# The gate's second product made of float32r parts in the large projections' banks

## The chip, the cores and the metric

The kernel runs on one core of a Trainium2 chip. The metric is the device time of one execution in microseconds (us). TensorE does matrix products, VectorE and ScalarE do elementwise work and read the products' banks (PSUM), GpSimd helps with elementwise work, and SyncE issues most of the loads. In the rows of the profile they are called PE, DVE, ACT, POOL and SP. PEld is TensorE's weight load.

## What is computed

Two layers of an encoder are applied to 768 rows (512 of one sequence, 256 of another) with a model width of 1024. Layer 0 runs differential attention and a bidirectional RWKV-7 mixer side by side, layer 1 runs dilated attention, and each layer ends with a SwiGLU network. The change touches one line of the RWKV mixer, the output gate g:

```python
GATE_LORA = 160
RWKV_WIDTH = RWKV_HEADS * HEAD_DIM          # 512

def rwkv_mixer(xn, r_p, k_p, v_p):
    ...
    xg = xn + xx * mu_g
    ...
    g = (jax.nn.sigmoid(xg @ g1) @ g2).astype(f32)
    ...
    return ((y + bonus.reshape(B, S, H * N)) * g).astype(xn.dtype)
```

The gate's hidden row has 160 columns. The kernel keeps them in two tiles, 128 of them in `hg` and 32 in `hh`, each with all 768 rows of the input along its free dimension.

## The kernel before

Large products are made of float32r parts. `split` makes two float32r tiles of a float32 tile: the high part is a cast on ScalarE (line 139), the low part is the remainder, a subtraction on VectorE (line 140). A product is then three float32r products, high by high, high by low and low by high. Small products are done in float32 directly (line 84).

A scheduler sets the order of each engine's instructions when the program is built. Line 83 gives every float32r product the lowest rank there is, so that it is put where nothing else is ready: it is filler. Each engine then works off its own list in order, and waits on semaphores for what it needs.

The work around the change is the method `rkv`, at about 20 to 365 us. For each of four blocks of 128 columns (j) it projects k, v and r, makes the operands of the RWKV recurrence in both directions (`operands`: tiles `AL`, `KB` and others, on VectorE, GpSimd and ScalarE), multiplies `AL` with `KB` in groups of 64x64 products (bank `pr`), and ScalarE copies the results to the tiles `G`. Each full `G` is inverted by `invert`: VectorE transposes it and solves 31 rows one after another (lines 752 and 754, here called the row chain), and TensorE makes 32x32 products in the bank `iv`, with ScalarE copies `Hs` and `Tif`/`Tib` between them. There are three such inversions. The last one needs the last `pr` products and is still running while the differential attention has begun.

`stage` makes the decays and rates of a block from their hidden tiles (bank `st`, one bank). `bonus` makes small products with `rk` (bank `pr`), which VectorE copies to `bon` (line 693). At the end of `rkv` come the gates' first projections (`gates`, names g and h), then `gate_out`, which makes g, and then `values`, which projects the values of the attention: six tiles of 24 float32r products in the banks `gm`, of which there are four. Weights go through five pairs of tiles `wh`/`wl` (`slot`) and two load tiles `wraw`.

After `rkv` follow the projections and scores of the differential attention (`diff_qk`, `diff_attention`), whose first product is a `gm<-xh,wh` at 365.45 us.

Of the kernel before, what the change touches and what calls it, by code (L numbers as in the profile page):

```python
# [18 lines left out]
P = 128  # L19
D = 1024  # L20
T = 768
# [33 lines left out]
class Core:  # L55
# [461 lines left out]
    def gate_out(self, hp, park):  # L517

        nc = self.nc
        g2b = self.pads[self.npad % 2][0:32, 0:512]  # L520
        nc.sync.dma_start(g2b, self.A["g2b"])
        for t in range(NT):
            o = self.bank("st")
            self.mm(o, self.hid["g"][:, t * P:(t + 1) * P], self.g2[0], True, False)
            self.mm(o, self.hid["h"][:, t * P:(t + 1) * P], g2b, False, True)
            g = self.big(("vv", "s", "sq")[t % 3])[:, 0:512]
            nc.scalar.copy(out=g, in_=o)
            nc.scalar.dma_start(park["g"][t], g)
# [1133 lines left out]
```

## Time and profile before

| | us |
|---|---|
| median of 3 runs | 2114.9 (2113.24 to 2115.16) |
| the profiled execution, device time | 2114.44 |
| the profiled execution, span of its instructions | 2112.6 |
| mean granted clock of TensorE over the span | 0.975 |

The device time is 1.8 us longer than the span from the first to the last instruction. The granted clock is a share of the full rate: 1.00 is 2.4 GHz, 0.50 is 1.2 GHz, and a value between them is a mean over a stretch that had both.

### The profile page before, as it was taken

Reading aid. Unit: us, or ns where it says so; the run is one execution under the profiler, and the core shown is the slowest. Engines: PE = TensorE matmul, PEld = TensorE weight load, DVE = VectorE, ACT = ScalarE, POOL = GpSimd, SP = SyncE. Lnnn points to the kernel's source line nnn. Section 1 sums busy time; section 2 is a strip of 40 time slices with the busy share of each in tenths; the row PEclk is TensorE's granted clock in tenths of the full one; section 3 lists DMA queues with packets and bytes.
Section 4 is the critical chain, followed back from the end, with each engine's and each line's share of the span. In section 5 each row is a group of like instructions: output and inputs, shape, how many; then the busy total and the mean of one; then the engine's idle time right before and its main releaser. Section 6 shows DMA issues by size and latency. Waiting matters only on the chain. (4 is left out here: it accounts for less than half of the span.)

```text
span 2112.6 us, 33740 instructions
## 1 busy us (share of the span) xinstructions
PE 2043.2 (97%) x13282; PEld 1768.4 (84%) x13282; DVE 1383.5 (65%) x2161; ACT 901.6 (43%) x1699; POOL 866.7 (41%) x819
## 2 busy tenths in 40 slices
PE   7999999999999999999999999999998999999998
PEld 7767676777887778999999998888687999999997
DVE  5456996846579577566666658544569566666665
ACT  5466565446655254433333335222445433333332
POOL 3344341543113137543443545553227434543442
PEclk9989997989999999999999999999899999999999
DMA  4334434214356212211122145320121222211124
GB/s 156 83 73 91 94 74 126 79 26 124 98 160 190 111 69 81 80 60 60 60 80 80 61 139 178 90 82 29 61 110 61 80 73 67 79 61 60 60 80 150
DMA packets 150227, 189.01 MB, mean 89 GB/s; under 512 B 95926, under 2 KB 107784, under 8 KB 150068
## 3 DMA queue, kind: packets, MB, share of 16 engines
q1 hardware_dynamic: 126880, 168.00, 25.6%
q10 hardware_dynamic: 20372, 12.03, 2.0%
q0 software_dynamic: 2816, 6.83, 1.1%
q8 instruction: 104, 1.70, 0.3%
q14 instruction: 55, 0.45, 0.1%
HBM read 150.20 MB, written 36.23 MB: 88 GB/s over the span
## 5 line engine op out<-in xcount | busy, mean ns | idle before, releaser
L83 PE MATMUL gm<-xh,w 128*128 128x384 f32 x864 | 236.1, 337 | 3.7 <-DVE sil L340 3.7
L140 DVE TENSOR_TENSOR wl<-wraw,wh 128x1024 fp32r<-128x1024 f32 (+1 forms) x96 | 125.5, 1308 | 156.3 <-ACT wh L139 153.2
L83 PE MATMUL gm<-T,w 128*128 128x384 f32 x1080 | 212.0, 339 | 6.1 <-DVE w L140 3.1
L83 PE MATMUL gm<-xh,wh 128*128 128x256 f32 (+3 forms) x640 | 207.9, 347 | 0.8 <-ACT pad L503 0.8
L83 PE MATMUL gm<-xl,wh 128*128 128x256 f32 (+3 forms) x640 | 206.7, 346 | 0.0
L83 PE MATMUL gm<-xh,wl 128*128 128x256 f32 (+3 forms) x640 | 205.3, 345 | 0.0
L83 PEld LDWEIGHTS gm<-T,w 128*128 128x128 f32 x1080 | 191.8, 188 | 11.9 <-DVE w L140 4.3
L140 DVE TENSOR_TENSOR w<-S,w 128x512 fp32r<-128x512 f32 x174 | 172.4, 991 | 40.9 <-ACT w L139 33.6
L139 ACT CAST wh<-wraw 128x1024 fp32r<-128x1024 f32 (+1 forms) x103 | 107.5, 1045 | 173.0 <-PE gm L83 103.1
L139 ACT CAST w<-S 128x512 fp32r<-128x512 f32 x174 | 107.8, 621 | 151.4 <-POOL S L299 56.7
L139 ACT CAST w<-wraw 128x512 fp32r<-128x512 f32 x126 | 76.0, 620 | 210.1 <-PE gm L83 141.3
L83 PEld LDWEIGHTS gm<-xh,w 128*128 128x128 f32 x864 | 158.1, 188 | 8.5 <-DVE sil L340 4.3
L83 PE MATMUL sc<-xh,w 128*128 128x384 f32 x544 | 150.5, 337 | 4.6 <-DVE xl L140 3.0
L140 DVE TENSOR_TENSOR w<-wraw,w 128x512 fp32r<-128x512 f32 x126 | 118.3, 955 | 41.3 <-ACT w L139 40.9
L303 POOL TENSOR_TENSOR S<-wraw,S 128x512 f32<-128x512 f32 x42 | 62.2, 1481 | 202.7 <-DVE w L140 202.7
L83 PE MATMUL gm<-xl,w 128*128 128x384 f32 x432 | 145.2, 336 | 0.0
L83 PEld LDWEIGHTS gm<-xh,wh 128*128 128x128 f32 (+1 forms) x640 | 119.7, 193 | 21.6 <-issue 5.8
L83 PEld LDWEIGHTS gm<-xh,wl 128*128 128x128 f32 (+1 forms) x640 | 118.9, 193 | 20.6 <-issue 7.4
L83 PEld LDWEIGHTS gm<-xl,wh 128*128 128x128 f32 (+1 forms) x640 | 119.0, 193 | 20.1 <-issue 7.7
L406 DVE TENSOR_TENSOR acc<-acc,ob 128x512 f32<-128x512 f32 x128 | 87.5, 684 | 63.4 <-PE ob L83 62.4
L358 POOL TENSOR_TENSOR sil<-sil,v 128x384 f32<-128x384 f32 x44 | 47.3, 1075 | 166.8 <-DVE v L340 166.4
L83 PE MATMUL ob<-wl,hh 128*128 128x512 f32 x288 | 113.5, 394 | 0.0
(511 smaller groups left out, 5279.6 us busy)
## 6 DMA issues: line engine op xcount, KB each, us to landing
wraw<-in_gate SPq DMA_DIRECT2D x44, 512.0 KB, 3.4
wraw<-in_down SPq DMA_DIRECT2D x44, 512.0 KB, 3.8
wraw<-in_up SPq DMA_DIRECT2D x40, 512.0 KB, 3.4
wraw<-in_wqk SPq DMA_DIRECT2D x20, 512.0 KB, 3.7
wraw<-in_wo SPq DMA_DIRECT2D x14, 512.0 KB, 4.1
wraw<-in_wrkv SPq DMA_DIRECT2D x12, 512.0 KB, 3.5
KB<-pkKB SPq DMA_DIRECT2D x24, 256.0 KB, 3.3
pkx<-x SPq DMA_DIRECT2D x12, 512.0 KB, 3.2
```

Source lines behind the costliest of these rows:

```text
L83: return self.nc.tensor.matmul(o, a, b, start=start, stop=stop)
L139: self.nc.scalar.copy(out=hi, in_=x)
L140: (eng or self.nc.vector).tensor_tensor(out=lo, in0=x, in1=hi.bitcast(F32), op=ALU.subtract)
L303: eng.tensor_tensor(out=s2, in0=a12, in1=s2, op=ALU.subtract)
L358: nc.gpsimd.tensor_tensor(out=o, in0=o, in1=a[0], op=ALU.mult)
L406: nc.vector.tensor_tensor(out=accs[t][:, fs], in0=accs[t][:, fs], in1=os[t, f], op=ALU.add)
```

## The change

`gate_out` splits the two hidden tiles and the two parts of the weight g2 into float32r parts, in three pairs of weight tiles, and makes each tile of g from six float32r products, in a bank `gm` and with the filler's rank, in place of two float32 products in the bank `st`. Copies and stores of g stay.

```diff
         g2b = self.pads[self.npad % 2][0:32, 0:512]
         nc.sync.dma_start(g2b, self.A["g2b"])
+        hg, hh, w = (self.slot() for _ in range(3))
+        self.split(*(x[:, :T] for x in hg), self.hid["g"])
+        self.split(*(x[:, 0:512] for x in w), self.g2[0])
+        self.split(*(x[0:32, :T] for x in hh), self.hid["h"])
+        self.split(*(x[0:32, 512:D] for x in w), g2b)
         for t in range(NT):
-            o = self.bank("st")
-            self.mm(o, self.hid["g"][:, t * P:(t + 1) * P], self.g2[0], True, False)
-            self.mm(o, self.hid["h"][:, t * P:(t + 1) * P], g2b, False, True)
+            o = self.bank("gm")
+            parts = [(h[a][:m, t * P:(t + 1) * P], w[b][:m, c:c + 512]) for h, m, c in ((hg, P, 0), (hh, 32, 512))
+                     for a, b in ((0, 0), (0, 1), (1, 0))]
+            for i, (a, b) in enumerate(parts):
+                self.mm(o, a, b, i == 0, i == len(parts) - 1)
             g = self.big(("vv", "s", "sq")[t % 3])[:, 0:512]
             nc.scalar.copy(out=g, in_=o)
             nc.scalar.dma_start(park["g"][t], g)
```

The scheduler makes a new order of it. Three places follow, with the tile written at the left of the arrow and those read at its right. The number behind a name is the tile's own.

TensorE, where the first projection of the gate h (`gm_3181`) ends. Before, the value projection (`gm_3299`) follows:

```order
L83 MATMUL gm_3181<-xl_90,wh_3176 64x256
L83 MATMUL gm_3181<-xh_89,wl_3177 64x256
L83 MATMUL gm_3299<-wh_3277,xh_89 128x512
L83 MATMUL gm_3299<-wl_3278,xh_89 128x512
L83 MATMUL gm_3299<-wh_3277,xl_90 128x512
```

With the change, `wh_3239`/`wl_3240` are the parts of hg, `wh_3241`/`wl_3242` those of hh, `wh_3243`/`wl_3244` those of g2:

```order
L83 MATMUL gm_3181<-xl_90,wh_3176 64x256
L83 MATMUL gm_3181<-xh_89,wl_3177 64x256
L83 MATMUL gm_3253<-wh_3243,wh_3239 128x512
L83 MATMUL gm_3263<-wh_3243,wh_3239 128x512
L84 MATMUL st_2686<-hw,w_492 128x512
L83 MATMUL gm_3253<-wl_3244,wh_3239 128x512
L83 MATMUL gm_3253<-wh_3243,wl_3240 128x512
L83 MATMUL gm_3263<-wl_3244,wh_3239 128x512
L83 MATMUL gm_3263<-wh_3243,wl_3240 128x512
L84 MATMUL iv_1552<-TS_1496,AO_852 32x32 x16
```

The products of g now stand first in this stretch, and the value projection starts behind all 36 of them.

TensorE, at the `pr` products of the last operand set (`AL_2705`, `KB_2707`). Before, the float32 products of g stand between them:

```order
L84 MATMUL iv_1642<-Tib_1499,Hs_1497 32x32 x16
L84 MATMUL pr_2727<-AL_2705,KB_2707 64x64 x6
L84 MATMUL st_3245<-g2a,hg 128x512
L84 MATMUL st_3245<-pad_280,hh 128x512
L84 MATMUL pr_2737<-AL_2705,KB_2707 64x64 x6
L84 MATMUL st_3251<-g2a,hg 128x512
L84 MATMUL st_3251<-pad_280,hh 128x512
L84 MATMUL pr_2747<-AL_2705,KB_2707 64x64 x6
```

With the change, the value projection (`gm_3337`, `gm_3365`, `gm_3393`) stands there:

```order
L84 MATMUL iv_1642<-Tib_1499,Hs_1497 32x32 x16
L84 MATMUL pr_2675<-AL_2625,KB_2627 64x64 x6
L83 MATMUL gm_3337<-wl_3328,xh_89 128x512
...
L83 MATMUL gm_3365<-wh_3333,xl_90 128x512
L84 MATMUL pr_2727<-AL_2705,KB_2707 64x64 x6
L83 MATMUL gm_3365<-wh_3333,xh_89 128x512
L83 MATMUL gm_3365<-wl_3334,xh_89 128x512
L83 MATMUL gm_3365<-wh_3333,xl_90 128x512
```

23 filler products follow `pr_2727` before the next `pr` group; before, two float32 products did.

VectorE, from the remainder of the last value weight (`wl_3296`) and the hidden tile hg on. Before:

```order
L140 TENSOR_TENSOR wl_3296<-wraw_3293,wh_3295 128x1024
L509 SCALAR_TENSOR_TENSOR hg<-s_3165,gm_3063 128x512
L509 SCALAR_TENSOR_TENSOR hg<-s_3165,gm_3064 128x256
L744 STREAM_TRANSPOSE M_2085<-G_1263 64x1024
L617 TENSOR_SCALAR kff_2629<-sa_2612,cols,omka 128x768
L622 TENSOR_TENSOR AL_2625<-kk_2433,E_2619 128x12x63
```

With the change (lines behind 522 are seven higher):

```order
L773 STREAM_TRANSPOSE tm_1391<-X_1390 64x1024
L509 SCALAR_TENSOR_TENSOR hg<-s_3165,gm_3063 128x512
L509 SCALAR_TENSOR_TENSOR hg<-s_3165,gm_3064 128x256
L751 STREAM_TRANSPOSE M_2085<-G_1263 64x1024
L140 TENSOR_TENSOR wl_3240<-hg,wh_3239 128x768
L140 TENSOR_TENSOR wl_3244<-g2a,wh_3243 128x512
L140 TENSOR_TENSOR wl_3244<-pad_280,wh_3243 32x512
L624 TENSOR_SCALAR kff_2629<-sa_2612,cols,omka 128x768
```

The remainders of hg and of the two parts of g2 stand behind hg now. The four remainders of the value weights, which stood ahead of hg, all stand further back.

## Rows read from the trace of the kernel before

**Rows 1.** The page: engine, busy time (share of the span) and instructions.

```profile
PE 2043.2 (97%) x13282; PEld 1768.4 (84%) x13282; DVE 1383.5 (65%) x2161; ACT 901.6 (43%) x1699; POOL 866.7 (41%) x819
```

**Rows 2.** Waits of TensorE, whole run: us in total, times, longest.

```profile
PE pr L84 <- DVE AL L623: 4.5, 2, 3.5
...
PE iv L84 <- ACT Hs L789: 2.9, 1, 2.9
```

**Rows 3.** Busy time of each engine in windows; then granted clock, DMA.

```profile
core 0: us, PE busy (x) PEld busy (x) DVE busy (x) ACT busy (x) POOL busy (x), PEclk, DMA share, GB/s
300.00:350.00 50.00, 48.92 (x287) 28.86 (x287) 37.87 (x75) 25.90 (x43) 16.40 (x15) 0.72 0.40 92
...
325.00:330.00 5.00, 5.00 (x15) 1.87 (x14) 4.83 (x7) 1.71 (x4) 1.03 (x2) 0.50 0.51 116
```

**Rows 4.** Timeline of TensorE, 312 to 353 us: start, duration, instruction, [idle before].

```profile
312.93 1.13 PE L84 MATMUL st<-g2a,hg 128*128 128x512 f32 x2
...
315.04 0.50 PE L83 MATMUL gm<-wh,xl 128*128 128x512 f32 x1
...
317.56 1.19 PE L84 MATMUL iv<-Tib,Hs 32*32 32x32 f32 x32
319.82 0.88 PE L84 MATMUL pr<-AL,KB 64*64 64x64 f32 x12 [1.07 <-DVE AL L623]
320.63 1.13 PE L84 MATMUL st<-g2a,hg 128*128 128x512 f32 x2
321.69 2.07 PE L84 MATMUL st<-pad,hh 32*128 32x512 f32 x2
323.69 1.54 PE L84 MATMUL pr<-AL,KB 64*64 64x64 f32 x12
325.16 2.07 PE L84 MATMUL st<-g2a,hg 128*128 128x512 f32 x2
...
340.11 1.91 PE L84 MATMUL iv<-TS,AO 32*32 32x32 f32 x32
341.95 2.72 PE L84 MATMUL pr<-rk,kfb 128*128 128x2 f32 x12
...
348.52 0.80 PE L83 MATMUL gm<-wh,xh 128*128 128x512 f32 x1
...
352.49 0.40 PE L83 MATMUL gm<-wh,xh 128*128 128x512 f32 x1
```

**Rows 5.** The same timeline: first value product, first product of the differential projections.

```profile
278.31 0.63 PE L83 MATMUL gm<-wh,xh 128*128 128x512 f32 x1
...
365.45 0.50 PE L83 MATMUL gm<-xh,wh 128*128 128x512 f32 x1
```

**Rows 6.** Timeline of VectorE, 271 to 345 us.

```profile
271.10 1.01 DVE L509 SCALAR_TENSOR_TENSOR hg<-s,gm 128x512 f32<-128x512 f32 x2
273.09 1.24 DVE L744 STREAM_TRANSPOSE M<-G 64x1024 f32<-64x1024 f32 x1 [0.98 <-ACT TS L784]
...
317.91 1.77 DVE L623 COPY AL<-kk 128x12 f32<-128x12 f32 x1
...
344.71 0.17 DVE L693 COPY bon<-pr 128x12 f32<-128x12 f32 x1 [10.61 <-PE pr L84]
```

**Rows 7.** Groups by line and form: busy us, mean ns of one, idle before.

```profile
L849 DVE TENSOR_TENSOR q<-q,q 64x768 fp32r<-64x768 f32 x1 | 1.0, 951 | 0.0
L140 DVE TENSOR_TENSOR w<-wraw,w 128x512 fp32r<-128x512 f32 x126 | 118.3, 955 | 41.3 <-ACT w L139 40.9
L752 DVE TENSOR_TENSOR tm<-X,M 128x322 f32<-128x322 f32 x2 | 1.0, 496 | 0.1
L139 ACT CAST w<-wraw 128x512 fp32r<-128x512 f32 x126 | 76.0, 620 | 210.1 <-PE gm L83 141.3
L613 ACT ACT_TABLE_LOAD x1 | 1.3, 1283 | 0.0
```

**Rows 8.** Timeline of TensorE, 421 to 431 us.

```profile
421.10 1.91 PE L84 MATMUL iv<-TS,AO 32*32 32x32 f32 x32 [2.85 <-ACT Hs L789]
...
430.90 0.42 PE L83 MATMUL gm<-xh,wl 128*128 128x512 f32 x1
```

## Prediction

> **What bounds the kernel now.** I read the page first: TensorE is busy for 97% of the span [rows 1], and over the whole run it is seldom named as waiting, for a few us each on VectorE or ScalarE [rows 2]. So the end moves when TensorE's instruction stream gets shorter, or when a wait or a slow clock is put into it. Then I took stretches by windows [rows 3]: from 300 to 350 us TensorE is busy nearly all the time, but its mean granted clock is 0.72, and inside, from 325 to 330 us, it is 0.50, the lower of the two levels (1.2 instead of 2.4 GHz). VectorE is busy for 38 of these 50 us, ScalarE for 26. Last, TensorE's timeline of this stretch [rows 4]: the gate's float32 products (`st<-g2a,hg` and `st<-pad,hh`, each recorded as two) stand in it in line with the `pr` products of the last operand set, and the clock falls while they run and is back at 352.49, 4 us after their end at 348.52, in a run of filler (`gm`).
>
> **What the order shows.** All 36 new products are filler and go to the front, into the time from 278 us on [rows 5], where the value projection (144 products) stood. The value projection moves back, between the `pr` products. Behind some 2,560 TensorE rows the two programs agree again but for a few neighbours, so what is won or lost before about 750 us should stay to the end.
>
> **Removed.** Six tiles of two float32 products, start to start [rows 4]: the first 2.11 us (312.93 to 315.04, full clock), the second 1.06 + 2.00, three more 12.0 (325.16 to 340.11 less two `pr` groups of 1.47), the last 4.0 (341.95 to 348.52 less 2.57 for the `rk` products). Together 21.2 us.
>
> **Added on TensorE.** 36 products of 128x512. Ten of that kind run from 315.04 to 317.56, 0.25 us each, so 9.0 us.
>
> **Clock given back.** At half clock a `pr` group takes 1.47 us instead of 0.81 (319.82 to 320.63), three times: 2.0. The `iv` group takes 1.84 instead of 1.2: 0.6. The `rk` products take 2.57, half of it lost: 1.3. Nine filler products from 348.52 to 352.49 take 3.97 instead of 2.25: 1.7. Together 5.6 us. If the lower clock goes with the float32 products, all of it returns. The sum on TensorE's work is -21.2 + 9.0 - 5.6 = -17.8 us.
>
> **New wait on VectorE.** The first `pr` product of the last operand set (pr_2727) needs `AL` from VectorE, which is done at 317.91 + 1.77 = 319.7 [rows 6]. TensorE was there at almost the same moment and waited 1.07 us. In the changed order the queue ahead of it is shorter. From 278.31 I count 81 filler products (20.3 us), six `iv` groups (7.2), four `pr` groups (3.2), one `rk` group (1.3) and four `st` products of the stage, two of 512 and two of 256 columns (3.2): 35.2 us, so TensorE arrives at 313.5. VectorE meanwhile gets more: the remainders of hg, hh and the two parts of g2. The nearest rows are 0.95 us for 768 elements and 0.96 for 512 [rows 7], so 3.8 us. Four remainders of the value weights move from ahead of hg to behind it, but stay ahead of `AL` and cancel. Six instructions of the row chain, 0.5 us each, go behind `AL`: -3.0. Net +0.8. The matrix transpose behind hg waited 0.98 us for ScalarE's copies out of the tile that it overwrites [rows 6], and the remainder that stood in front of it is gone, so I add 1.0. That gives `AL` at 321.5, with 317.5 (the other short gaps absorbed) and 327 (the new rows at twice their price, as when they collide with GpSimd) as bounds. TensorE waits 8.0 us there in place of 1.1: +6.9 (+3 to +12). Behind it in TensorE's queue stand the value projection and everything after it.
>
> **Clock after that wait.** After 348.52 it was back 4 us later, 1.7 us of them lost. With one `pr` group I take 2.0 (0 to 5).
>
> **ScalarE.** Two casts of 512 columns at 0.62 us [rows 7], two of 768 at about 0.9 (scaled), and the order puts a sigmoid between the two exponentials of the last set, which makes two more table loads of 1.28 us: 5.6 us on an engine that is free for half of this stretch [rows 3]; hidden there. Without that cover it would delay `AL` by up to as much, which the bound of 327 holds. I add 1.0 us (0 to 3) for `pr` and `iv` products that find ScalarE's copies later than their shorter queue. Copies out of the banks and stores of g are the same six, and the load of g2b is the same one on SyncE's queue: 0.
>
> **At the first differential projection** (365.45 before [rows 5]) the sum is -17.8 + 6.9 + 2.0 + 1.0 = -7.9 us.
>
> **Further on.** At 421.10 TensorE waits 2.85 us for a ScalarE copy between two `iv` groups, and the clock is low until 430.90 [rows 8]: of those 9.8 us about 4.9 are lost, 7.7 with the wait. The changed order has 35 filler products and a transpose between these two groups, where 23 stood, some 3 us more, which just covers the wait. But VectorE's row chain ahead of them starts no earlier than now, since it needs the last `pr` products, so TensorE may wait for it instead. I take a third: -2.5 (0 to -7.7).
>
> **Sum.** -7.9 - 2.5 = -10.4, and 0.4 back because 0.25 us also holds the start of a run: -10. The profiled execution took 2114.44 us (span 2112.6); the median of the runs is 0.5 above it. Forecast: 2104.4 us.
>
> **Rivals.** (1) *Nothing is taken back.* VectorE is early (its gaps are absorbed) and the wait at 421 vanishes. For it: VectorE's own load ahead of `AL` grows by only 0.8 us. Against it: TensorE reaches pr_2727 six us before VectorE did even in the kernel before. -17.8 + 3 - 2 = -16.8, about 2098.
> (2) *The gain is swallowed.* TensorE runs ahead, and each later place where it meets VectorE's chain for the last inverse takes the lead away: it starts when ScalarE has copied the last `pr` group, and between the first and the fourth `pr` group now stand 71 filler products (17.8 us) where 11.1 us of float32 stood (3.06 + 2 x 4.0). For it: VectorE stood idle for 10.61 us until 344.71 for just these products [rows 6], and I see it start at the same time or up to 3 us later. Against it: behind that point the order gives TensorE more filler ahead of the inverse's products than before. Left is 0 to 3 us, about 2113.
> (3) *Slower: the clock stays low.* Bursts of filler now alternate with small float32 products and waits from 278 us on. If every burst starts at the lower level and none gets out of it, the 99 filler products behind pr_2727 cost 0.44 instead of 0.25 us (+18.8), and the small groups between them (9.3 us) double: +28. With -12 for the rest (the sum without the 2.0 of the clock) it ends at +16, 2130. It decides against the change from about 12 us lost, that is, if the clock is low for 24 us. For it: that is what the float32 stretch did for 30 us. Against it: the clock was back at 352.49, in the first run of filler behind the float32 products [rows 4], and here 23 such products (5.8 us at full clock) stand between two `pr` groups. The Trainium skill (TensorE: Matmul & The Clock Gate, HAM oscillation) describes such a loop, where each wait throttles the array again and every burst begins at the half rate. By that rule the time would be the 2130 of this rival. The trace agrees on how a burst begins (the product at 278.31 has 0.63 us in its row [rows 5], the first at 348.52 has 0.80 [rows 4]), not on its staying there.
>
> **How the numbers follow.** Forecast 0.60 (own range 2099 to 2109), rival 1 0.15, rival 2 0.18, rival 3 0.07. The range of 2096.5 to 2111.5 holds the forecast, most of rival 1 and the lower edge of rival 2; the bounds of the `AL` time and of the 421 us wait add up to about the same width. A change of 0.2% (4.2 us) is about what a measurement of this kernel can tell from none. Faster than that: the forecast, rival 1 and a sixth of rival 2, 0.78. Within it: most of rival 2, 0.15. Slower: 0.07.
>
> **What would show it.** In the changed profile: 36 `gm` products on split gate operands between 278 and 300 us; no float32 product in a bank `st` after the stage products; a wait of TensorE for VectorE's `AL` of about 8 us near 320; the granted clock near 1 from 330 to 357; the first differential projection at 356 to 359. The prediction is wrong if `AL` comes after 327, if the clock stays at 0.5 through the value projection, or if the lead at 357 is gone by 460 us.

## The result: slower by 0.6%

| | before | changed |
|---|---|---|
| median of 5 runs, us | 2113.24 (2107.73 to 2115.16) | 2124.16 (2122.76 to 2128.35) |
| span of the profiled execution, us | 2112.6 | 2121.0 |
| mean granted clock over the span | 0.975 | 0.974 |

The ratio is 1.0059 (95% interval 1.004 to 1.0077): 11 us slower, where I forecast 10 us faster. The page of the changed kernel answers to [rows 1]:

```profile
span 2121.0 us, 33784 instructions
...
PE 2044.1 (96%) x13294; PEld 1775.5 (84%) x13294; DVE 1385.4 (65%) x2165; ACT 908.3 (43%) x1705; POOL 868.6 (41%) x819
```

TensorE is as busy as before (2044.1 us to 2043.2), so the products saved nothing that can be seen here, and most of what the span grew by is time in which it is idle. To see where, I laid two marks: the **first mark** is the first product `cf<-Xs,Ti` of the recurrence, the **second mark** the first transpose `sc<-ident,xn` behind the output projection. Windows between them, the first split at the first `sc<-Xs,Ti`, the second at the last row of products of `Xs` and `Ti`. Before (columns as in [rows 3]):

```profile
506.04:603.90 97.86, 96.69 (x1307) 80.53 (x1308) 58.42 (x143) 60.70 (x164) 15.83 (x47) 1.00 0.39 110
603.90:693.30 89.40, 81.39 (x1310) 70.22 (x1308) 80.89 (x136) 43.82 (x93) 27.88 (x18) 0.98 0.61 180
693.30:737.71 44.41, 41.36 (x231) 33.64 (x229) 22.99 (x34) 9.50 (x23) 9.38 (x15) 0.92 0.33 125
737.71:2112.60 1374.89, 1346.04 (x7273) 1218.86 (x7271) 878.76 (x1206) 509.47 (x915) 606.50 (x539) 0.99 0.24 80
```

Changed (and first the time at the lower level in the front):

```profile
271.70:322.90 51.20, 50.60 (x293) 35.73 (x290) 37.15 (x96) 30.84 (x52) 10.80 (x8) 0.50 0.43 113
504.44:604.40 99.96, 96.96 (x1303) 80.79 (x1302) 59.65 (x142) 60.49 (x162) 15.90 (x47) 1.00 0.40 109
604.40:710.30 105.90, 93.04 (x1362) 80.57 (x1361) 78.87 (x137) 45.13 (x94) 27.66 (x18) 0.94 0.52 151
710.30:746.34 36.04, 33.85 (x179) 27.70 (x178) 21.72 (x32) 9.34 (x22) 7.82 (x13) 1.00 0.40 141
746.34:2121.00 1374.66, 1345.53 (x7273) 1218.00 (x7271) 882.37 (x1206) 509.54 (x915) 608.77 (x542) 0.99 0.24 81
```

The last 1375 us are the same in both. At the first mark the changed kernel is 1.6 us ahead (504.44 to 506.04). Between the marks it needs 241.9 us where before needed 231.7 (97.86 + 89.40 + 44.41). So the front gained 1.6 us and not 10, and 10.2 us were lost in a stretch that the prediction never costed.

**The front.** TensorE's timeline of the changed kernel from 270 us on, where before the value projection was about to begin [rows 5]:

```profile
270.60 1.19 PE L84 MATMUL iv<-TS,AO 32*32 32x32 f32 x32 [3.27 <-ACT Hs L796]
272.39 1.54 PE L84 MATMUL pr<-AL,KB 64*64 64x64 f32 x12 [0.60 <-ACT AO L669]
...
275.20 1.05 PE L83 MATMUL gm<-wh,wh 128*128 128x512 f32 x2
276.19 2.07 PE L84 MATMUL st<-hw,w 64*128 64x512 f32 x2
278.19 0.79 PE L83 MATMUL gm<-wl,wh 128*128 128x512 f32 x1
278.78 0.63 PE L83 MATMUL gm<-wh,wl 128*128 128x512 f32 x1
279.21 0.63 PE L83 MATMUL gm<-wl,wh 128*128 128x512 f32 x1
...
280.19 1.91 PE L84 MATMUL iv<-TS,AO 32*32 32x32 f32 x32
...
286.53 0.80 PE L83 MATMUL gm<-wh,wh 128*128 128x512 f32 x1
...
322.75 1.26 PE L84 MATMUL iv<-Tib,Hs 32*32 32x32 f32 x32
...
331.85 0.88 PE L84 MATMUL pr<-AL,KB 64*64 64x64 f32 x12
...
368.26 0.51 PE L83 MATMUL gm<-xh,wh 128*128 128x512 f32 x1 [0.17 <-ACT sq L833]
```

The products of g (`gm<-wh,wh` and so on) come where I put them, from 275 us on, two, four and six at a time between small groups. But all of them run at the lower level: next starts are 0.43 us apart (278.78 to 279.21) in place of 0.25. The clock fell at 271.7, in the first group behind a wait of 3.27 us, and came back at 322.9; by then all 36 products of g were done and a run of 11 value products had been made. The product `pr` on the last `AL` waits for nothing (331.85), for VectorE finishes that `AL` just ahead of it, at 331.71. VectorE's timeline, changed:

```profile
306.14 0.18 DVE L631 COPY dc<-E 128x12 f32<-128x12 f32 x1 [8.11 <-ACT E L620]
...
330.43 0.93 DVE L629 TENSOR_TENSOR AL<-kk,E 128x756 f32<-128x756 f32 x1
331.29 0.42 DVE L630 COPY AL<-kk 128x12 f32<-128x12 f32 x1
```

The first of these rows is the longest wait of VectorE on the way there: 8.11 us for ScalarE's exponential `E`. ScalarE's timeline, changed and then before:

```profile
298.08 0.59 ACT L534 COPY vv<-gm 128x512 f32<-128x512 f32 x1 [3.64 <-PE gm L83]
...
305.26 0.84 ACT L620 ACTIVATE E<-sw 128x768 f32<-128x768 f32 x1
```

```profile
295.80 0.85 ACT L613 ACTIVATE E<-sw 128x768 f32<-128x768 f32 x1 [0.51 <-DVE sw L612]
```

In the changed order three copies of g stand ahead of `E` on ScalarE, and the first of them waits 3.64 us for its products. `E` comes 9.5 us later than before.

### The profile page after: what moved, and what is told of

Its sections match the earlier page's. It is cut to its first block, busy times and chain, and to the rows that moved or that the text cites. A ratio compares the mean times of both kernels' runs of the same rounds, so it can differ in the third digit from the quotient of the medians.

```text
span 2121.0 us, 33784 instructions
## 1 busy us (share of the span) xinstructions
PE 2044.1 (96%) x13294; PEld 1775.5 (84%) x13294; DVE 1385.4 (65%) x2165; ACT 908.3 (43%) x1705; POOL 868.6 (41%) x819
## 5 line engine op out<-in xcount | busy, mean ns | idle before, releaser
L83 PE MATMUL gm<-xh,w 128*128 128x384 f32 x864 | 235.9, 337 | 3.7 <-DVE sil L340 3.7
```

Source lines behind the costliest of these rows:

```text
L83: return self.nc.tensor.matmul(o, a, b, start=start, stop=stop)
```

## The experiments

One account is used for the front. The first mark, less half of the time at the lower level ahead of it, less TensorE's idle time ahead of it, is the work at the full clock: 506.0 - 78.5/2 - 28.3 = 438.4 us before, 504.4 - 78.5/2 - 29.7 = 435.5 changed. The stretch is the time between the marks. Each number is one profiled execution; ratios are of five rounds (three for the pair with one load) to the kernel before on the same chip. The profiled executions lie up to 4.9 us from the median of their kernel's runs, and runs of the kernel before went from 2098.95 to 2119.21 us, so differences of less than 5 us between single rows say little. The account takes idle time at the lower level off one and a half times. Counted once, the work is 439.4 before, 436.1 changed and 438.4 for the change with the values first.

| kernel | ratio (95%) | first mark | lower level ahead | work | stretch |
|---|---|---|---|---|---|
| before | | 506.0 | 78.5 | 438.4 | 231.7 |
| changed | 1.0059 (1.004 to 1.0077) | 504.4 | 78.5 | 435.5 | 241.9 |
| float32 in gm | 1.0009 (0.9995 to 1.0022) | 504.2 | 75.1 | 433.7 | 230.9 |
| splits alone | 1.0027 (1.0012 to 1.0042) | 500.5 | 61.4 | 439.4 | 241.6 |
| stacked | 0.996 (0.9946 to 0.9974) | 496.0 | 68.3 | 431.7 | 229.7 |
| stacked, values first | 1.0012 (1.0002 to 1.0023) | 491.1 | 51.2 | 429.4 | 246.7 |
| the same, remainders on GpSimd | 0.9944 (0.9924 to 0.9964) | 493.2 | 54.6 | 432.4 | 236.6 |
| change, values first | 0.9957 (0.9941 to 0.9974) | 500.0 | 71.7 | 435.9 | 231.4 |
| parts in st | 1.0018 (1.0001 to 1.0036) | 503.9 | 75.1 | 434.7 | 236.8 |
| change, weights a step later | 1.0047 (1.0032 to 1.0063) | 507.2 | 85.3 | 434.8 | 242.4 |
| change, one load | 1.0026 (1.0011 to 1.004) | 507.2 | 85.3 | 435.3 | 235.9 |
| before, one load | 1.0035 (1.0012 to 1.0058) | 505.9 | 78.5 | 438.6 | 239.7 |
| values first alone | 1.0023 (1.0006 to 1.0041) | 499.4 | 64.9 | 438.4 | 242.4 |

The work column sorts the kernels by what makes g: 438.4 to 439.4 with float32 products, 434.7 to 435.9 with 36 parts, 429.4 to 432.4 with 24 products. The exception is float32 in gm, 433.7, whose order and idle time ahead of the mark (32.9 us) differ from the others; it lies below the kernels with 36 parts, so the sorting is no proof.

**1. The banks alone.**

```diff
-            o = self.bank("st")
+            o = self.bank("gm")
             self.mm(o, self.hid["g"][:, t * P:(t + 1) * P], self.g2[0], True, False)
```

> The kernel before with one word changed: the float32 products of g stay, but in the banks gm in place of the bank st. It has no splits and no new products. Two marks are read in every run here: the first product cf<-Xs,Ti of the recurrence (506.0 us before, 504.4 with the change) and the first transpose sc<-ident,xn behind the output projection (737.7 before, 746.3 with the change). Theory A (the change's loss of about 10 us comes between these marks, from the order in which the last recurrence steps and the casts of the output projection's weights stand on the engines, which is not the change's own work): the order between the marks is here almost that of before, so the stretch takes 231.7 us plus or minus 3, not 241.9. Theory B (the loss comes from the gate's products and what they delay): nothing is said against the banks, so 2113 plus or minus 4 as well, but by B the stretch between the marks has no reason to follow the order. Both: total 2109 to 2117; low clock from about 321 us for some 30 us, as before.

2112.39 us, ratio 1.0009: the same as before, with a stretch of 230.9. The lower level came earlier than expected (273.0 to 290.0 and 296.9 to 313.9), where the float32 products of g stand in this kernel (274.9 to 310.3). The banks cost nothing that can be measured. The second fall stands behind no wait of TensorE. Windows ahead of it and from it on (columns as in [rows 3]), and the row of TensorE's timeline just ahead of it, four float32 products on the 32 rows of `hh`:

```profile
289.95:296.90 6.95, 6.95 (x57) 3.56 (x55) 6.95 (x32) 4.15 (x7) 0.00 (x0) 0.99 0.00 0
296.90:313.95 17.05, 17.05 (x64) 8.42 (x63) 16.40 (x37) 8.01 (x14) 3.14 (x3) 0.50 0.65 170
```

```profile
293.27 3.69 PE L84 MATMUL gm<-pad,hh 32*128 32x512 f32 x8
```

**2. The splits alone.**

```diff
+        hg, hh, w = (self.slot() for _ in range(3))
+        self.split(*(x[:, :T] for x in hg), self.hid["g"])
+        self.split(*(x[:, 0:512] for x in w), self.g2[0])
+        self.split(*(x[0:32, :T] for x in hh), self.hid["h"])
+        self.split(*(x[0:32, 512:D] for x in w), g2b)
         for t in range(NT):
             o = self.bank("st")
```

> The kernel before with the change's four splits added (casts on ScalarE, remainders on VectorE, three weight slots) and nothing that reads them; g is still made by float32 products. Theory B (the splits delay VectorE and ScalarE and so the last inverse): the first mark, cf<-Xs,Ti, comes 3 us or more later than the 506.0 of before. Theory A: the first mark within 2 us of 506.0, and the time between the two marks (231.7 before, 241.9 with the change) goes by the order there, which in this kernel is neither that of before nor that of the change: between 229 and 244. Total by A 2111 to 2125, by B 2116 and more.

Neither theory had the first mark: 500.5, 5.5 us earlier than before, with about 1 us more of work and 17.1 us less at the lower level. Theory B falls: the splits delay nothing there. The stretch is 241.6 and the total 2118.2, although nothing reads the splits and g is made as before. So a kernel gets the 10 us without any of the products of the change. Its trace also shows float32 products of g at the full clock. TensorE's timeline:

```profile
328.57 0.91 PE L84 MATMUL pr<-AL,KB 64*64 64x64 f32 x12
329.41 1.13 PE L84 MATMUL st<-g2a,hg 128*128 128x512 f32 x2
330.46 1.12 PE L84 MATMUL st<-pad,hh 32*128 32x512 f32 x2
331.51 0.91 PE L84 MATMUL pr<-AL,KB 64*64 64x64 f32 x12
332.35 1.13 PE L84 MATMUL st<-g2a,hg 128*128 128x512 f32 x2
...
338.83 1.19 PE L84 MATMUL iv<-TS,AO 32*32 32x32 f32 x32
341.51 2.07 PE L84 MATMUL st<-g2a,hg 128*128 128x512 f32 x2 [1.49 <-ACT s L532]
343.52 2.07 PE L84 MATMUL st<-pad,hh 32*128 32x512 f32 x2
```

and its windows there:

```profile
296.40:340.70 44.30, 43.63 (x301) 28.98 (x299) 41.99 (x71) 22.07 (x38) 14.78 (x12) 1.00 0.48 115
340.70:351.00 10.30, 9.49 (x17) 5.32 (x18) 5.42 (x28) 7.92 (x11) 3.56 (x5) 0.50 0.39 128
```

Five of six tiles of g are made by float32 products between `pr` groups, with no filler between the last of them, and the clock stays up. It falls beside a wait of 1.49 us, and the sixth tile takes the 4.0 us that four of six took before. In [rows 4] too a wait (1.07 us, ahead of 319.82) stands just before the fall at 321.7. So float32 products of g do not bring the lower level wherever they stand. They are not cleared either: in experiment 1 the clock fell at 296.9 in a run of them and of small groups, with no wait, and stayed low while the last four stood there.

**3. Fewer products.** The three products on the 32 rows of `hh` become one on 96 rows (part of the diff to the kernel before).

```diff
+        (x, y), hid = hh, self.hid["h"]
+        for z, s, n, hi, lo in ((x, hid, T, (0, 64), 32), (y, g2b, 512, (0, 32), 64)):
+            for p in hi:
+                nc.scalar.copy(out=z[p:p + 32, :n], in_=s)
+            nc.vector.tensor_tensor(out=z[lo:lo + 32, :n], in0=s, in1=z[0:32, :n].bitcast(F32), op=ALU.subtract)
...
+            self.mm(o, x[0:96, ts], y[0:96, 0:512], False, True)
```

> The change, but the three float32r products on the 32 rows of hh are stacked into one product of 96 rows (high, low and high part of hh above each other, against high, high and low of the weights): 24 products instead of 36. Between the marks (first cf<-Xs,Ti, first sc<-ident,xn) the order is almost that of the kernel before. Theory A: the stretch between the marks takes 232 plus or minus 3 us. The first mark comes at 504.4 less 12 products, which ran for 0.43 us each at the low clock: 499 to 504. Total 2105 to 2112, so 2 to 8 us faster than before. Theory B (the loss of the change is the gate's products' own doing, in the front or through the last inverse): two thirds of the products are left, so two thirds of the loss of 11 us: 2120 plus or minus 2.

2102.91 us, ratio 0.996, the first kernel that beats both. The stretch, with almost the order of before (about one in ten of some 805 TensorE rows stands elsewhere), is 229.7; the first mark, 496.0, and the total are 3 and 2 us better than expected. Theory B, which wanted 2120, falls.

**4. The value projection first, as before.** Against experiment 3:

```diff
-        self.gate_out(hp, park)
         self.values(xh, xl, park)
+        self.gate_out(hp, park)
```

> As the kernel with stacked products, but the value projection is called ahead of the gate's second stage, so that its 144 products stand first again as in the kernel before. Between the marks the order of TensorE, VectorE and ScalarE is word for word that of the changed kernel. Theory A: the stretch between the marks takes 242 plus or minus 2 us, 10 more than before, whatever the front does. Theory C (a refinement: the low clock of 51 us from 271.7 us came because four banks gm were held by half-made tiles of g while the parts of hh were not ready, so the filler came in bursts of 4 to 6 products between small groups, where the value projection had bursts of 9 to 10): with the value projection in front the clock is up until about 320 and low for less than 35 us between 270 and 360, and the first mark comes at 490 to 500; without C it comes at 500 to 504. Total by A and C 2107 to 2117, by A alone 2117 to 2121. Theory B (the products of g delay what follows): 2113 or less, with a stretch between the marks of some 232.

The front gains most of all: the first mark is at 491.1, and between 260 and 370 us the clock is low for 23.9 us (54.6 in the changed kernel). And the order between the marks, word for word that of the changed kernel on TensorE, VectorE and ScalarE, takes all of it back:

```profile
260.00:370.00 110.00, 96.93 (x836) 77.05 (x834) 91.39 (x208) 67.04 (x107) 34.34 (x28) 0.89 0.44 118
491.09:590.50 99.41, 96.80 (x1307) 80.75 (x1306) 59.70 (x142) 60.46 (x164) 15.41 (x47) 1.00 0.39 109
590.50:698.60 108.10, 95.92 (x1362) 82.94 (x1361) 79.42 (x137) 45.11 (x94) 27.25 (x18) 0.91 0.51 148
698.60:737.82 39.22, 37.03 (x180) 30.00 (x178) 22.07 (x33) 9.33 (x22) 8.90 (x15) 0.91 0.39 141
```

246.7 us, with 17.0 us of idle TensorE (18.0 changed, 12.2 before). That is 2.7 us over the expected range; the clock was low for 27.3 us in it (13.7 changed). The total, 2114.3, is that of a kernel 15 us ahead at the first mark and 15 us slower between the marks.

**5. The same front with the other order.** Against experiment 4:

```diff
-        self.split(*(x[:, :T] for x in hg), self.hid["g"])
-        self.split(*(x[:, 0:512] for x in w), self.g2[0])
+        self.split(*(x[:, :T] for x in hg), self.hid["g"], nc.gpsimd)
+        self.split(*(x[:, 0:512] for x in w), self.g2[0], nc.gpsimd)
```

> The kernel with stacked products and the value projection first, and the remainders of hg and g2a on GpSimd in place of VectorE. The order between the two marks is nearly that of the kernel before again (130 of 805 TensorE rows differ, where all but a few did in the kernel with the remainders on VectorE). Theory A (the stretch between the marks goes by the order in it): 231 plus or minus 3 us, with the first mark where the kernel with VectorE's remainders had it, at 491 plus or minus 4: total 2094 to 2102. Rival R (the stretch gets longer because the front gets there earlier, and something behind it does not come earlier): 246 as in that kernel, total 2110 to 2116.

2100.64 us, ratio 0.9944. The first mark is where it was (493.2), and the stretch drops from 246.7 to 236.6, 2.6 us above the expected range. Rival R, which wanted 246, falls: a kernel that gets there early keeps most of its lead if the order is nearly that of before. The remainders that changed engines are made more than 150 us ahead of the stretch.

**6. The change with the values first.** The diff of experiment 4, on the change with its 36 products.

> The change as it is, with all 36 products of g, but the value projection called ahead of the gate's second stage. Between the marks the order is nearer to before (325 TensorE rows differ) than to the changed kernel (888). Theory A: stretch 232 plus or minus 4. Theory C (value projection in front in bursts of 17 keeps the clock up): low clock between 260 and 370 us under 35 us in place of 54.6; first mark 3 to 5 us behind the 491 of the stacked one, 493 to 498. Total by A and C 2099 to 2106. Without A the stretch takes 242 to 247 and the total is 2110 to 2120; without C the first mark is at 502 to 506.

2103.71 us, ratio 0.9957. Two lines swapped turn a ratio of 1.0059 into one of 0.9957: the stretch is 231.4, and the clock is low for 34.1 us between 260 and 370. The first mark, 500.0, is 2 us later than expected.

**7. The products where the float32 ones were.**

```diff
-            o = self.bank("gm")
+            o = self.bank("st")
             parts = [(h[a][:m, t * P:(t + 1) * P], w[b][:m, c:c + 512]) for h, m, c in ((hg, P, 0), (hh, 32, 512))
```

> The change, but the products of g go to the one bank st, so that they stand in sixes between the last pr groups, where the float32 products stood, and the value projection is in front of them. Theory C: the clock is up from 300 us on, low for less than 35 us between 260 and 370, and the first mark at 494 to 502. If the low clock went with the products of g and not with the short bursts of filler, it is low around them as before (320 to 350) and the first mark at 502 to 506. The order between the marks is neither that of before nor that of the changed kernel, so by theory A the stretch can take anything from 228 to 247, and the total 2097 to 2122.

A miss for theory C: the clock was low for 51.2 us (from 271.0 to 294.9 and from 315.4 to 342.7) and the first mark at 503.9. The value projection starts only at 290.0 in this kernel, and from 276 to 290 small groups follow each other without filler. So the first fall is not the doing of the products of g: here the low time lasts from 271 to 295 before the first of them (310.6). The second, from 315.4, does stand over the last four of the six tiles, and the first mark is the 502 to 506 of the rival, by which the low clock goes with those products.

**8. The change with the output projection's weights one step later.**

```diff
-SO = 9
+SO = 10
```

> The changed kernel with one number changed that has nothing to do with the gate: the output projection's weights are called behind the tenth step of the recurrence and not the ninth. Its front is that of the change. Between the marks the first half of the order, with the early casts on ScalarE, stays that of the changed kernel, and only the second half differs from it (203 TensorE rows; 711 from before). Theory A1 (the early casts, which wait for their loads ahead of the recurrence's copies, cost the 10 us): stretch 239 to 246, total 2119 to 2125. Theory A2 (the second half of the order does): 230 to 236, total 2109 to 2115. First mark 504 plus or minus 2 by both.

2121.11 us, ratio 1.0047, stretch 242.4, which is A1's number, though the first mark, 507.2, is 1.2 us later than expected. The number came another way: the clock was low for 23.9 us in the stretch (13.7 changed). Less half of that, 230.4 us are left, where the changed kernel has 235.1 and the one before 226.6, so this run does not clear the second half of the order. The casts of those weights do stand earlier on ScalarE with the change. Its timeline, changed:

```profile
605.85 1.56 ACT L139 CAST xh<-wraw 128x768 fp32r<-128x768 f32 x2 [1.53 <-DMA pko<-oT]
...
610.67 0.83 ACT L139 CAST xh<-wraw 128x768 fp32r<-128x768 f32 x1 [1.89 <-DMA wraw<-pko]
...
616.08 1.04 ACT L139 CAST wh<-wraw 128x1024 fp32r<-128x1024 f32 x1 [2.01 <-DMA wraw<-in_wo]
...
618.77 1.05 ACT L139 CAST wh<-wraw 128x1024 fp32r<-128x1024 f32 x1 [1.34 <-DMA wraw<-in_wo]
```

and before:

```profile
612.32 0.83 ACT L139 CAST xh<-wraw 128x768 fp32r<-128x768 f32 x1 [2.34 <-DMA wraw<-pko]
...
622.38 1.03 ACT L139 CAST wh<-wraw 128x1024 fp32r<-128x1024 f32 x1
```

The casts wait for their loads at the head of ScalarE's queue, with copies of the recurrence behind them. Experiments 9 and 10 asked whether these waits are the price.

**9 and 10. Without the loads.** In layer 0 one tile of the output projection's weights stands for all eight, so its output is not the model's. On the change, and on the kernel before:

```diff
-        return [C.weights(A[f"wo{L}"][i], slot=slot(i), eng=None if L else nc.gpsimd) for i in range(n)]
+        if L:
+            return [C.weights(A[f"wo{L}"][i], slot=slot(i)) for i in range(n)]
+        r, out = C.raw(A["wo0"][0]), []
+        for i in range(n):
+            h, l = slot(i) or C.slot()
+            C.split(h, l, r, nc.gpsimd)
+            out.append((h, l))
+        return out
```

> The changed kernel, with the first tile of the output projection's weights loaded once and used in place of all eight, so that the eight casts on ScalarE never wait for a load (the output projection multiplies with the wrong weights, in the same number of products). The last recurrence steps, from the first to the last product with Xs and Ti in the banks sc and ob, take 89 to 93 us in kernels with the order of before and 102 to 108 in those with that of the change. Theory D1 (the casts, put early, wait for their loads ahead of the recurrence's copies on ScalarE): this stretch falls to 88 to 95 us, and the total to 2108 to 2114. Theory D2 (the order of the recurrence steps themselves costs it, the waiting casts only stand in idle time): 100 us or more, total 2117 to 2123.

> The kernel before with the same edit (one tile of the output projection's weights for all eight). Its ScalarE waits there for loads only 6 us in all. Theory D1: the last recurrence steps take 85 to 92 us, within 3 us of the changed kernel with this edit, total 2107 to 2114. Theory D2: 88 to 92 us, 10 or more below the changed kernel with this edit.

Neither theory has both numbers. In the changed kernel the recurrence's last steps went from 105.9 to 94.0 us, as D1 said (the total, 2116.45, stayed above its range). But in the kernel before they went from 89.4 to 107.5, although ScalarE waits there for a load only once, for 2.0 us. (These lengths also hold products of the output projection, 52 more of them in the changed kernel than before, as the windows above count; the stretch is the better measure: 235.9 and 239.7.) The trace of experiment 10 shows where its time went. VectorE, GpSimd and TensorE there, in order of time:

```profile
615.58 0.41 DVE L1029 TENSOR_TENSOR S<-S,dc 128x256 f32<-128x256 f32 x1
...
637.51 8.02 POOL L140 TENSOR_TENSOR xwl<-wraw,xwh 128x1024 fp32r<-128x1024 f32 x3
...
640.77 2.56 DVE L1029 TENSOR_TENSOR S<-S,dc 128x256 f32<-128x256 f32 x1
...
643.82 0.47 PE L84 MATMUL ob<-SUV,LK 128*64 128x64 f32 x2 [6.30 <-ACT SUV L1010]
```

With nothing to load for them, GpSimd makes the eight remainders nearly one behind another (623.07 to 645.53). VectorE's operation took 2.56 us beside them in place of 0.41, and TensorE's longest wait in the stretch, 6.30 us, hangs on its result by way of a ScalarE copy. The next, 4.43 us at 628.87, is for a load of the recurrence's own `RH`. The kernel before has no wait above 3.1 us between the marks. So experiment 10 lost its time to what the edit put there and says nothing of the waits for the weights in the changed kernel; these stay a candidate, as the edit took 6.0 us off its stretch.

**11. The swap alone.** The diff of experiment 4 on the kernel before.

> The kernel before with the value projection called ahead of the gate's second stage and nothing else: g is still made by float32 products in the bank st. Is the gain of the swapped change (first mark 500.0, 506.0 before) the swap's or the parts'? If the parts' work counts (36 products of 0.25 us for 12.7 us of float32 at the full clock, 3.7 us) and the clock is the same, the first mark comes 3 to 4 us behind the swapped change: 503 to 505, and no sooner than 500 even if the clock is down for 10 us less. If the swap alone makes the gain, 500 plus or minus 1. The order between the marks is neither that of before nor that of the change, so the stretch may take 230 to 245, and the total 2106 to 2121.

First mark 499.4: the swap gains as much in the front as the swapped change did, through 13.6 us less at the lower level, and the work stays at 438.4. That is the second case of the expectation, the swap's gain and not the parts'. The stretch is 242.4, the total 2116.62, ratio 1.0023. So the swap without the parts is slower than before, and with them faster, and both times the stretch decides.

## Why the prediction was wrong

- **Removed, 21.2 us: right as a row, wrong as a gain.** It was mostly the price at the lower level. At the full clock a tile takes 2.11 us (as the first in [rows 4]), six take 12.7, so the work that the change saves is 12.7 - 9.0 = 3.7 us. Measured in the work column: 438.4 - 435.5 = 2.9.
- **Added, 9.0 us: mis-sized.** They took 17.6 us (0.99 + 2.00 + 2.86 + 5.41 + 6.31, start to start), all at the lower level.
- **Clock given back, 5.6 us: the step that failed.** "If the lower clock goes with the float32 products, all of it returns": it did not go. From 262 us to the first differential projection the time at the lower level grew from 34.1 to 54.6 us, so the clock took 10.2 us more there (half of 20.5) and gave nothing back. It stood from 271.7 to 322.9, on the new products, where before it stood from 321.7 to 352.4. That both kernels have 78.5 us of it ahead of the first mark is an accident: before, 20.5 ahead of 262 us, 34.1 and then 23.9; changed, 13.7, 54.6 and 10.2. Experiment 2 shows float32 products at the full clock, experiment 7 the lower level without any product of g. What holds the clock down stays open (experiment 1).
- **New wait on VectorE, +6.9: did not come, and `AL` was mis-timed.** `AL` was done at 331.7, beyond my bound of 327. The step that failed there is "hidden there" for ScalarE, and the 0 for the copies of g: they stand ahead of the exponential `E`, and VectorE waited 8.11 us for it. TensorE was no earlier than `AL`, as it was slowed by the clock. Whether it would have waited for `AL` at the full clock is not shown. With the 2.0 and 1.0 us next to it, this is the part of the sum that the lower clock replaced.
- **First differential projection:** forecast 356 to 359, measured 368.26, 2.8 us later than before. From there to the first mark 4.4 us came back, with 13.7 us less at the lower level.
- **Further on:** the wait at 421 came back as 2.34 us at 434.28. The low time there shrank from 10.2 to 3.4 us. So this term had the right sign. At the first mark 2.9 us of work less 1.4 us more of idle time (29.7 to 28.3) leave 1.5 of the 1.6 us.
- **"What is won or lost before about 750 us should stay": right behind 750, and it hid the rest.** The order of the two programs differs until then, and I costed nothing of it behind 431 us. Between the marks 10.2 us were lost: 5.8 of idle TensorE, 1.7 (half of 3.4) of lower clock, and 2.7 that is spread over longer busy time.
- **The rivals.** Rival 3 had the sign (2130, chance 0.07) and its first half: bursts of filler between small groups, at the lower level for 51.2 us. The Trainium skill (TensorE: Matmul & The Clock Gate, HAM oscillation) describes waits that throttle the array again, so that bursts start slow. The trace agrees that the clock falls beside a wait at 271.7, though the first group behind that wait still ran at the full clock (1.19 us at 270.60), and the clock did return at 322.9. But the low clock is not what made the kernel slower at the first mark, where both had 78.5 us of it. Rival 2 had the front nearly right (0 to 3 us left), by another way.

What stays open is which moved instruction costs the 10 us between the marks. That the order there does it rests on this: an order near that of before gave 229.7 to 236.6 us (experiments 1, 3, 5, 6), that of the change or nearly that 241.9 to 246.7 (the change, 4, 8), with fronts of every kind. The others gave 235.9 to 242.4, experiment 10 among them (239.7), whose order is nearer to that of before than to that of the change; so nearness alone is no rule, and the two groups lie only 5.3 us apart. Experiments 4 and 5 differ by an edit more than 150 us ahead of the place. The same order also brings the same waits. TensorE in the changed kernel and then in experiment 4:

```profile
628.98 1.01 PE L84 MATMUL sc<-SUV,KBT 128*64 128x64 f32 x13 [2.72 <-DVE SUV L1029]
```

```profile
617.49 0.90 PE L84 MATMUL sc<-SUV,KBT 128*64 128x64 f32 x13 [2.72 <-DVE SUV L1032]
```

A wait of 2.62 us ahead of `ob<-Xs,Ti` (607.73 and 593.77) and one of 1.50 ahead of `tr<-ident,o` also stand in both; the kernel before and experiment 3 have neither, and share one of 1.19 and 1.15 us for a load of `RH` (615.64 and 605.01). Two candidates are seen and not tried by themselves. One is the early casts on ScalarE, with their waits for loads. The other is GpSimd's remainders of the same weights, which come earlier too: in the changed kernel the 2.72 us stand behind a VectorE operation of 2.82 us (625.64) beside two of them (625.57 to 630.67), of a kind that takes 0.69 elsewhere (631.19). Also not tried is whether half-made tiles of g, holding the four banks `gm` until the parts of `hh` are ready, made the filler come in such short runs; that was only argued.

## What to carry to other kernels

Price what is removed at the clock that it would have without the disturbance, and ask what the clock fell for before counting it as given back: here a wait stood beside three falls (271.7, 321.7, and 340.7 in experiment 2), another (296.9 in experiment 1) had none, and whatever stood behind the fall paid. Where a scheduler makes the order, a change is not over where its own instructions end: compare the orders to the place where they agree again, and treat every stretch up to there as a term of the sum with its own uncertainty, here some 17 us from the shortest to the longest (229.7 to 246.7). A time that comes out wrong is then no verdict on the idea: the same 36 products, called behind the values, gave 0.9957. Nor is that number one for it: the swap alone had the front as early (499.4 to 500.0) and lost by the stretch.

## What the runs showed of the hardware that was not expected

A float32 product of 512 columns, recorded as two, took 1.05 us from start to start at the full clock (329.41 to 330.46) and 2.0 at the lower (341.51 to 343.52), in the same kernel. A series of such products and of small groups from 328.57 to 338.83, with no filler in it, left the granted clock at 1.00. In the changed kernel dense filler from 304.56 to 313.30 ran at 0.50 and the clock was back only at 322.9, while before it was back 4 us into a run of filler. Six of the twelve products of g in that stretch had 32 rows; whether that matters was not tried. The clock also fell with TensorE busy throughout: at 296.9 in experiment 1 (6.95 of the 6.95 us ahead of it). A VectorE operation on 128x256 took 2.56 us beside a remainder on GpSimd, and 0.41 us elsewhere in the same stretch (experiment 10, 640.77 and 615.58).
